# Sparse attention over latent vectors: keys and values of each head made first, scores over 64 rows, values mixed straight into a head's rows

## The chip, the core and the metric

The kernel runs on one NeuronCore of a Trainium2 chip. Its engines are TensorE (PE in the profile; its weight loads are PEld), VectorE (DVE), ScalarE (ACT), GpSimd (POOL) and SyncE (SP), whose queue issues most of the loads. Each engine works through a list of its own, in order, and waits for others by semaphores. The metric is the device time of one execution in microseconds: the median of three timed runs. One execution more is recorded with the hardware profiler, and the profile is of that one.

## The reference

The model has a first block (two layers with differential and grouped attention, feed-forward parts, and a context stream) and a second block of two layers, each with three branches side by side: a sparse attention over latent vectors, a stick-breaking attention and a matrix memory, then gates and a projection. There are 256 tokens and 1024 features, all fp32. The change is in the sparse attention alone. It has 8 heads of 64 features, of which the first 16 are rotated by position; keys and values of all heads come from one latent vector of 128 features per token. Of the keys a query may see, a separate small scoring chooses 64:

```python
def dsa_attention(q, c_kv, k_rope, iq, ik, iw, w_uk, w_uv, kv_norm_w, cos, sin):
    topk = min(INDEX_TOPK, seq // 4)                      # 64
    c_kv = rms_norm(c_kv, kv_norm_w)                      # the latent vectors, rank 128
    q_rope = partial_rope(q[..., :ROPE_DIM], cos[:, None], sin[:, None])
    q_nope = q[..., ROPE_DIM:]
    k_rope = partial_rope(k_rope, cos, sin)
    ...
    q_abs = jnp.einsum('bshn,rhn->bshr', q_nope, w_uk)
    q_cat = jnp.concatenate([q_abs, q_rope], axis=-1).astype(jnp.float32) * DSA_HEAD_DIM ** -0.5
    kv_cat = jnp.concatenate([c_kv, k_rope], axis=-1).astype(jnp.float32)

    def block(args):                                      # 128 queries
        ...
        score = jnp.einsum('bth,bths->bts', iwb, jax.nn.relu(jnp.einsum('bthd,bsd->bths', iqb, ik)))
        score = jnp.where(causal[None], score, -jnp.inf)
        _, sel = lax.top_k(score, topk)
        kv_sel = jax.vmap(lambda kv, ix: kv[ix])(kv_cat, sel)
        logits = jnp.einsum('bthf,btkf->bthk', qb, kv_sel)
        logits = jnp.where(valid[:, :, None, :], logits, -jnp.inf)
        p = jax.nn.softmax(logits, axis=-1)
        return jnp.einsum('bthk,btkr->bthr', p, kv_sel[..., :DSA_KV_RANK])

    o_lat = from_blocks(lax.map(block, ...))
    o = jnp.einsum('bshr,rhv->bshv', o_lat, w_uv)
```

## The kernel before

The second block holds features on the partitions and 256 tokens along the free axis. Every projection is made of three fp32r products per weight tile (`mm3`, L78 to L80), from a high and a low part of weight and input; `unit` makes the two parts of a weight (L60, `wh`, on ScalarE, and L61, `wl`, on VectorE) from a tile `raw` that SyncE's queue loads. `pair` makes two such units into one PSUM bank `psp`. Matmuls of the attention itself are plain fp32; in the profile each of them is two instructions of one kind, and the transposes are one each.

`hybrid(l)` is one layer. The attention's part has these steps. Narrow projections come first (`kz`, `iq`), with the rope on VectorE and GpSimd (`rope`, L439 to L442). `index_bias` makes for each half t of the queries the mask `sc` (0 for a chosen key, -1e30 elsewhere): scores `psI` (L1047), then eight rounds of MAX8 and MATCH_REPLACE8 on VectorE (L1058, L1059). Then the latent vectors `ckT` (L889 to L896, normed by `psR`) and their transpose `ckt` (`psct`, L899); the queries `dq` (two `pair`s, L902 to L907, scaled on ScalarE at L905, then the rope); and the transposed up-projections of the keys, `ukT` (`psuk`, L916).

For each cp, that is four heads, the queries are brought into the latent space: `qa` (`psqa`, L926, copied by ScalarE at L930). For each half t of the queries, with nk = 128 (t + 1) keys, the scores `psL` are a sum of two matmuls: 128 rows of `qa` against `ckT` (L940), and 64 rows of `dq` against the rotated part `kR` (L941). The index e in 0, 1 is the half of the 128 rows that a head occupies. The softmax follows: add the mask (L946), maximum (L947), exp on ScalarE (L950), reciprocal (L951), scale (L952). The probabilities are transposed (`psdt`, L958), copied by ScalarE (`dPT`, L960) and mixed with the latent vectors (`psol`, L961, 512 columns), copied by VectorE (`olat`, L963); at the end of each cp the mix goes through the up-projection of the values (`psya`, L968, two heads in two halves of the array's columns).

The order on each engine is not the order of the program: a scheduler deals the instructions out by its own costs, and fills the gaps of the attention with products of the later projections (`sbq`, `sbk`, `sbv` and others). PSUM has eight banks of 512 fp32 columns, shared out by tags in `PSUM_TAGS`: "p" two (`psp`), "s" two (`psL`, `psI`, `psol` and others), "a" one, "b" three. A new tile of a tag waits until a bank of it is read out. SBUF tiles have tags in the same way.

## Time and profile before

| | |
|---|---|
| median of three timed runs | 2602.63 us (2601.14 to 2602.85) |
| profiled execution, first to last instruction (its span) | 2598.3 us |
| TensorE busy | 2500.7 us (96%), 15175 matmuls |
| VectorE, ScalarE, GpSimd busy | 1435.2, 1038.1, 406.3 us |
| mean granted clock of TensorE | 0.984 of 2.4 GHz |
| read from HBM | 343.04 MB, 132 GB/s over the span |

The page gives no other time of the profiled execution than its span. Busy is the union of an engine's instructions; a matmul's length includes its way through the array, so successive matmuls overlap, and their cost is read from start to start. The second block begins at about 1885 us; the sparse attention of its layer 0 runs from about 1900 to 1993 us, that of layer 1 from about 2254 to 2347 us.

### The profile page before, as it was taken

The numbers are of one execution on the slowest core, as the hardware profiler recorded it, in microseconds if no ns is written. First come the engines' busy times: TensorE is split into PE (matmuls) and PEld (weight loads), VectorE is DVE, ScalarE is ACT, GpSimd is POOL, SyncE is SP. The second block draws the span as 40 slices with busy tenths as digits, with TensorE's granted clock in tenths as the row PEclk, the third lists the DMA queues.
The fourth block names the chain that finished last, engine by engine and source line by source line (L and its number), as shares of the span: only waits on it lengthen the run. The fifth ranks groups of instructions, "written<-read, shape, count | busy, mean of one in ns | idle before, by whom it ended". The sixth has DMA issues, their size and how long they took to land. (4 is left out here: it accounts for less than half of the span.)

```text
span 2598.3 us, 38082 instructions
## 1 busy us (share of the span) xinstructions
PE 2500.7 (96%) x15175; PEld 2105.4 (81%) x15175; DVE 1435.2 (55%) x2492; ACT 1038.1 (40%) x1740; POOL 406.3 (16%) x427
## 2 busy tenths in 40 slices
PE   7999999999999999999999999999989999899998
PEld 3777778666678888788888887799887999788998
DVE  4333337666565333474333477656785765676755
ACT  3222234554353222343222355644444544446443
POOL 1000016220051000150000153400330010201010
PEclk9999998999999999999999999999999999999999
DMA  8443423344432322243332243455533356433453
GB/s 282 153 154 129 147 97 99 126 148 150 149 116 86 107 97 97 98 146 114 114 101 94 98 155 125 143 182 180 161 105 113 106 158 194 140 98 114 138 187 130
DMA packets 321789, 346.56 MB, mean 133 GB/s; under 512 B 23906, under 2 KB 282568, under 8 KB 321612
## 3 DMA queue, kind: packets, MB, share of 16 engines
q1 hardware_dynamic: 320706, 343.35, 40.9%
q8 instruction: 119, 1.95, 0.3%
q10 hardware_dynamic: 906, 0.78, 0.1%
q14 instruction: 58, 0.48, 0.1%
HBM read 343.04 MB, written 1.05 MB: 132 GB/s over the span
## 5 line engine op out<-in xcount | busy, mean ns | idle before, releaser
L60 ACT CAST wh<-raw 128x1024 fp32r<-128x1024 f32 (+2 forms) x534 | 527.8, 998 | 1120.7 <-PE psg L79 554.1
L61 DVE TENSOR_TENSOR wl<-raw,wh 128x1024 fp32r<-128x1024 f32 (+2 forms) x534 | 639.4, 1203 | 549.0 <-ACT wh L60 547.0
L79 PE MATMUL psg<-xl,wh 128*128 128x512 f32 (+1 forms) x1472 | 523.6, 356 | 3.1 <-POOL xl L1295 3.0
L78 PE MATMUL psg<-xh,wh 128*128 128x512 f32 (+1 forms) x1472 | 523.3, 357 | 2.9 <-ACT xh L1322 2.3
L80 PE MATMUL psg<-xh,wl 128*128 128x512 f32 (+1 forms) x1472 | 521.4, 355 | 0.0
L78 PE MATMUL psp<-xh,wh 128*128 128x256 f32 x1248 | 357.2, 287 | 10.0 <-DVE mlu L1156 3.8
L80 PE MATMUL psp<-xh,wl 128*128 128x256 f32 x1248 | 354.5, 284 | 3.1 <-DVE wl L61 3.1
L79 PE MATMUL psp<-xl,wh 128*128 128x256 f32 x1248 | 356.7, 286 | 0.6 <-POOL xl L855 0.6
L78 PEld LDWEIGHTS psg<-xh,wh 128*128 128x128 f32 x1472 | 277.3, 189 | 59.0 <-ACT wh L60 12.6
L79 PEld LDWEIGHTS psg<-xl,wh 128*128 128x128 f32 x1472 | 278.2, 189 | 53.1 <-issue 8.1
L80 PEld LDWEIGHTS psg<-xh,wl 128*128 128x128 f32 x1472 | 278.0, 189 | 39.7 <-issue 0.8
L79 PE MATMUL psy<-gl,wh 128*128 128x512 f32 (+1 forms) x800 | 273.8, 342 | 2.6 <-DVE gl L323 2.5
L78 PE MATMUL psy<-gh,wh 128*128 128x512 f32 (+1 forms) x800 | 275.2, 344 | 0.0
L80 PE MATMUL psy<-gh,wl 128*128 128x512 f32 (+1 forms) x800 | 273.6, 342 | 0.0
L78 PEld LDWEIGHTS psp<-xh,wh 128*128 128x128 f32 x1248 | 237.3, 190 | 16.3 <-issue 5.7
L80 PEld LDWEIGHTS psp<-xh,wl 128*128 128x128 f32 x1248 | 237.6, 191 | 5.4 <-DVE wl L61 4.1
L79 PEld LDWEIGHTS psp<-xl,wh 128*128 128x128 f32 x1248 | 237.9, 191 | 4.1 <-issue 2.4
L243 POOL TENSOR_TENSOR acc<-acc,sq 128x256 f32<-128x256 f32 x70 | 56.9, 816 | 1108.2 <-ACT acc L237 1102.5
L319 DVE TENSOR_TENSOR g<-sg,psg 128x512 f32<-128x512 f32 (+1 forms) x88 | 54.5, 620 | 223.4 <-PE psg L80 223.4
L78 PEld LDWEIGHTS psy<-gh,wh 128*128 128x128 f32 x800 | 150.3, 188 | 26.4 <-ACT wh L60 5.0
L79 PEld LDWEIGHTS psy<-gl,wh 128*128 128x128 f32 x800 | 151.1, 189 | 22.7 <-DVE gl L323 3.2
L80 PEld LDWEIGHTS psy<-gh,wl 128*128 128x128 f32 x800 | 150.5, 188 | 21.6 <-issue 1.7
(473 smaller groups left out, 3651.6 us busy)
## 6 DMA issues: line engine op xcount, KB each, us to landing
raw<-in_ffn_w_in SPq DMA_DIRECT2D x88, 1024.0 KB
raw<-in_w_in SPq DMA_DIRECT2D x70, 1024.0 KB
adaw<-in_ada_w SPq DMA_DIRECT2D x240, 256.0 KB
raw<-in_ffn_w_out SPq DMA_DIRECT2D x32, 1024.0 KB
adas<-in_ada_w SPq DMA_DIRECT2D x48, 256.0 KB
raw<-in_ffn_w_out SPq DMA_DIRECT2D x16, 768.0 KB
raw<-in_da_w_in SPq DMA_DIRECT2D x12, 1024.0 KB
raw<-in_w_branch SPq DMA_DIRECT2D x24, 512.0 KB
```

The lines of the kernel that those rows point to most:

```text
L60: a = nc.scalar.copy(wh[:, 0:nk, :], r)
L61: b = nc.vector.tensor_sub(wl[:, 0:nk, :], r, wh[:, 0:nk, :].bitcast(F32))
L78: mm(ps, lhsT=wh[:, k, :], rhs=xh, start=first, stop=False)
L79: mm(ps, lhsT=wh[:, k, :], rhs=xl, start=False, stop=False)
L80: mm(ps, lhsT=wl[:, k, :], rhs=xh, start=False, stop=last)
L243: b = (eng or nc.vector).tensor_tensor(acc, acc, sq, ALU.add)
L319: nc.vector.tensor_mul(g[:, 0:width], sg[:, 0:width], pu[:, 0:width])
```

## The change

The latent vectors are no longer transposed, and queries are no longer brought into the latent space. Instead, right after `ckT` is ready, the keys of every head are made from it, `kd` (`pskd`, four matmuls of 256 columns); the weights `uk` have 16 zero columns in front of each head's 48, and VectorE adds the rotated part `kR` on its way out of PSUM, so that a head has 64 rows, two heads side by side on the 128 partitions. The values of all heads are made too, tokens on the partitions, `vd` (`psvd`, two matmuls of 512 columns, copied by ScalarE). A score `psL` is then one matmul over 64 rows. The mix goes from the transposed probabilities `PT` straight into the 64 rows of a head in `psya` (matmuls of 128 columns), for one or two blocks of keys, and one copy `ya` per cp remains. `pskd` and `psvd` take the tag "a" (one bank, with `psdt`), `psya` the tag "b". The loads of `uk` and `uv` stand before the queries' projections. The changed file also has no comments; its lines in the attention are some 7 to 14 lower.

```diff
-for _t, _n in (("p", "psp psckv"), ("s", "psL psI psR psRn psst psol"), ("a", "psrot psvec psiw psct psuk psqa psdt psya psf"),
-               ("b", "psk2 pstk psz psC psyb pscm psmS psn psyc psgt")):
+for _t, _n in (("p", "psp psckv"), ("s", "psL psI psR psRn psst psol"), ("a", "psrot psvec psiw pskd psvd psdt psf"),
+               ("b", "psk2 pstk psz psC psyb pscm psmS psn psyc psgt psya")):
...
-               ("d", "kz iq kR sc csq ck dq qa olat dPT ya"), ("e", "sbq sbk sbv sbvt yb"), ("m", "mlu mlth mlv wt hn yc"),
-               ("th", "th tho uk ukT"), ("E", "rl dE"), ("br", "bh bl"), ("mg", "mg"), ("z", "z")):
+               ("d", "kz iq kR sc csq ck dq kd vd dPT ya"), ("e", "sbq sbk sbv sbvt yb"), ("m", "mlu mlth mlv wt hn yc"),
+               ("th", "th tho uk"), ("E", "rl dE"), ("br", "bh bl"), ("mg", "mg"), ("z", "z")):
...
-        ck = self.t2("ck")
-        ckT, ckt = ck[:, 0:256], ck[:, 256:512]
+        ckT = self.t2("ck")[:, 0:256]
         nc.scalar.activation(ckT, psc[:, 0:256], AF.Identity, scale=self.col['kv_norm'][:, l:l + 1])
         nc.vector.tensor_tensor(ckT, ckT, R[:, 0:256], ALU.mult)
-        pt = self.pst("psct")
+
+        uk = self.t2("uk").rearrange("p (h n) -> p h n", n=64)
+        nc.gpsimd.memset(uk[:, :, 0:16], 0.0)
+        nc.sync.dma_start(uk[:, :, 16:64], I['w_dsa_uk_2'][l])
+        uv = self.big.tile([128, 512], F32, name="uv", tag="uv")
+        nc.sync.dma_start(uv, I['w_dsa_uv_2'][l].rearrange("r h v -> r (h v)"))
+        kd, vd = [], []
+        for cp in range(2):
+            ps = self.pst("pskd")
+            for i in range(2):
+                c = 2 * cp + i
+                nc.tensor.matmul(ps[:, i * 256:(i + 1) * 256], lhsT=uk[:, 2 * c:2 * c + 2, :].rearrange("p a b -> p (a b)"), rhs=ckT)
+            t = self.t2("kd")
+            nc.vector.tensor_tensor(v2(t), v2(ps), kR.unsqueeze(1).to_broadcast([128, 2, 256]), ALU.add)
+            kd.append(t)
         for t in range(2):
-            nc.tensor.transpose(pt[:, t * 128:(t + 1) * 128], ckT[:, t * 128:(t + 1) * 128], self.ident)
-        nc.vector.tensor_copy(ckt, pt[:, 0:256])
+            ps = self.pst("psvd")
+            nc.tensor.matmul(ps, lhsT=ckT[:, t * 128:(t + 1) * 128], rhs=uv)
+            v = self.t2("vd")
+            nc.scalar.copy(v, ps)
+            vd.append(v)
         dq = []
...
-        # up-projections of the keys, transposed, 16 zero rows in front of each head
-        uk = self.t2("uk").rearrange("p (h n) -> p h n", n=64)
-        nc.gpsimd.memset(uk[:, :, 0:16], 0.0)
-        nc.sync.dma_start(uk[:, :, 16:64], I['w_dsa_uk_2'][l])
-        uv = self.big.tile([128, 8, 64], F32, name="uv", tag="uv")
-        nc.sync.dma_start(uv, I['w_dsa_uv_2'][l])
-        pt = self.pst("psuk")
-        for c in range(4):
-            nc.tensor.transpose(pt[:, c * 128:(c + 1) * 128], uk[:, 2 * c:2 * c + 2, :].rearrange("p a b -> p (a b)"), self.ident)
-        ukT = self.t2("ukT")
-        nc.scalar.copy(ukT, pt)
         ya = []
         for cp in range(2):
-            qa = {}
-            ps = [self.pst("psqa") for e in range(2)]      # the two halves of the rows write different banks
-            for i in range(2):
-                for e in range(2):
-                    r = slice(64 * e, 64 * e + 64)
-                    nc.tensor.matmul(ps[e][:, i * 256:(i + 1) * 256], lhsT=ukT[r, (2 * cp + i) * 128:(2 * cp + i + 1) * 128],
-                                     rhs=dq[cp][r, i * 256:(i + 1) * 256])
-            for e in range(2):
-                t = self.t2("qa")
-                nc.scalar.copy(t, ps[e])
-                qa[e] = t
-            ol = [self.t2("olat") for c in range(2)]       # heads 4cp, 4cp+1 | 4cp+2, 4cp+3
+            po = self.pst("psya")
...
-                        nc.tensor.matmul(L[e][:, i, :], lhsT=qa[e][:, qs], rhs=ckT[:, 0:nk], start=True, stop=False)
-                        nc.tensor.matmul(L[e][:, i, :], lhsT=dq[cp][r, qs], rhs=kR[r, 0:nk], start=False, stop=True)
+                        nc.tensor.matmul(L[e][:, i, :], lhsT=dq[cp][r, qs], rhs=kd[cp][r, i * 256:i * 256 + nk])
...
-                po = self.pst("psol")
+                PT = []
                 for st in range(t + 1):
                     pt = self.pst("psdt")
                     for h in range(4):
                         nc.tensor.transpose(pt[:, h * 128:(h + 1) * 128], E[h % 2][:, h // 2, st * 128:(st + 1) * 128], self.ident)
-                    PT = self.t2("dPT")
-                    nc.scalar.copy(PT, pt)
-                    nc.tensor.matmul(po, lhsT=ckt[:, st * 128:(st + 1) * 128], rhs=PT, start=st == 0, stop=st == t)
-                for c in range(2):
-                    nc.vector.tensor_copy(v2(ol[c])[:, :, t * 128:(t + 1) * 128],
-                                          po[:, c * 256:(c + 1) * 256].rearrange("p (e q) -> p e q", q=128))
-            ps = self.pst("psya")
-            for cc in range(2):
-                for e in range(2):
-                    nc.tensor.matmul(ps[64 * e:64 * e + 64, cc * 256:(cc + 1) * 256], lhsT=uv[:, 4 * cp + 2 * cc + e, :],
-                                     rhs=ol[cc][:, e * 256:(e + 1) * 256])
+                    PT.append(self.t2("dPT"))
+                    nc.scalar.copy(PT[st], pt)
+                for i in range(2):
+                    for st in range(t + 1):
+                        for e in range(2):
+                            h = 2 * i + e
+                            nc.tensor.matmul(po[64 * e:64 * e + 64, i * 256 + t * 128:i * 256 + t * 128 + 128],
+                                             lhsT=vd[st][:, (4 * cp + h) * 64:(4 * cp + h + 1) * 64], rhs=PT[st][:, h * 128:(h + 1) * 128],
+                                             start=st == 0, stop=st == t)
             t = self.t2("ya")
-            nc.scalar.copy(t, ps)
+            nc.scalar.copy(t, po)
```

The scheduler deals the changed work out anew. TensorE, layer 1, from where the latent vectors are ready: before, the new queries stand between products and the scores follow them (`psct` and `psuk` are some rows ahead).

```order
L80 MATMUL psp_20820<-xh3_20137,wl_20822 128x256
L926 MATMUL psqa_20611<-dq_20526,ukT_20609 128x256 x2
L78 MATMUL psp_20820<-xh4_20138,wh_20821 128x256
L79 MATMUL psp_20820<-xl4_20146,wh_20821 128x256
L80 MATMUL psp_20820<-xh4_20138,wl_20822 128x256
L78 MATMUL psp_20820<-xh5_20139,wh_20821 128x256
L79 MATMUL psp_20820<-xl5_20147,wh_20821 128x256
L80 MATMUL psp_20820<-xh5_20139,wl_20822 128x256
L926 MATMUL psqa_20612<-dq_20526,ukT_20609 128x256 x2
L940 MATMUL psL_20623<-ck_20460,qa_20617 128x128
L941 MATMUL psL_20623<-kR_20311,dq_20526 128x128
L940 MATMUL psL_20623<-ck_20460,qa_20617 128x128
```

After the change, the keys and values stand at this place:

```order
L79 MATMUL psp_20519<-xl6_20113,wh_20524 128x256
L907 MATMUL pskd_20433<-ck_20425,uk_20428 128x256 x2
L80 MATMUL psp_20519<-xh6_20105,wl_20525 128x256
L78 MATMUL psp_20519<-xh7_20106,wh_20524 128x256
L79 MATMUL psp_20519<-xl7_20114,wh_20524 128x256
L80 MATMUL psp_20519<-xh7_20106,wl_20525 128x256
L907 MATMUL pskd_20438<-ck_20425,uk_20428 128x256 x2
L913 MATMUL psvd_20443<-uv_20431,ck_20425 128x512
L913 MATMUL psvd_20447<-uv_20431,ck_20425 128x512
L78 MATMUL psp_20750<-xh0_20099,wh_20751 128x256
L79 MATMUL psp_20750<-xl0_20107,wh_20751 128x256
```

Four products stand between the two `pskd`, none between `pskd_20438` and the two `psvd`; `psp_20750`, the next projection, begins behind them, and the scores come 22 products later.

ScalarE, layer 1, the same place: before, the queries `dq_20526` are taken out of their bank among the weights' high parts.

```order
L60 CAST wh_20821<-raw_20818 128x1024
L905 ACTIVATE dq_20526<-psp_20469 128x512
L60 CAST wh_20825<-raw_20818 128x1024
L60 CAST wh_20882<-raw_20879 128x1024
L60 CAST wh_20886<-raw_20879 128x1024
L905 ACTIVATE dq_20592<-psp_20535 128x512
L918 COPY ukT_20609<-psuk_20604 128x512
L930 COPY qa_20617<-psqa_20611 128x512
L930 COPY qa_20619<-psqa_20612 128x512
```

After the change, both copies of the values stand ahead of both queries:

```order
L60 CAST wh_20751<-raw_20748 128x1024
L60 CAST wh_20755<-raw_20748 128x1024
L60 CAST wh_20812<-raw_20809 128x1024
L60 CAST wh_20816<-raw_20809 128x1024
L915 COPY vd_20445<-psvd_20443 128x512
L915 COPY vd_20449<-psvd_20447 128x512
L921 ACTIVATE dq_20510<-psp_20453 128x512
L921 ACTIVATE dq_20576<-psp_20519 128x512
L60 CAST wh_20873<-raw_20870 128x1024
```

What moved: `dq_20510` (bank `psp_20453`) is now behind `vd_20449`, which needs the second `psvd`.

VectorE, layer 1, after `psR`: before, the rope of the first queries (L440, L442) stands among the rounds of the mask.

```order
L227 TENSOR_SCALAR dg_20457<-ident_88,rs_20451 128x128
L1058 MAX m8_20354<-sc_20324 128x8
L440 TENSOR_TENSOR trot_20528<-trot_20528,cs2_16255 128x512
L1059 MATCH_REPLACE sc_20324<-m8_20354,sc_20324 128x128
L896 TENSOR_TENSOR ck_20460<-ck_20460,psR_20453 128x256
L1058 MAX m8_20357<-sc_20324 128x8
L442 TENSOR_TENSOR dq_20526<-dq_20526,trot_20528 128x512
L1059 MATCH_REPLACE sc_20324<-m8_20357,sc_20324 128x128
L900 COPY ck_20460<-psct_20463 128x256
L1058 MAX m8_20360<-sc_20324 128x8
L61 TENSOR_TENSOR wl_20822<-raw_20818,wh_20821 128x1024
```

After the change, from the first to the second sum of the keys:

```order
L909 TENSOR_TENSOR kd_20436<-pskd_20433,kR_20276 128x512
L1049 MAX m8_20325<-sc_20289 128x8
L1167 SCALAR_TENSOR_TENSOR fg_20286<-one4_16262,ex_21799 4x256
L1050 MATCH_REPLACE sc_20289<-m8_20325,sc_20289 128x128
L61 TENSOR_TENSOR wl_20817<-raw_20809,wh_20816 128x1024
L1049 MAX m8_20328<-sc_20289 128x8
L1049 MAX m8_20352<-sc_20289 128x8
L1050 MATCH_REPLACE sc_20289<-m8_20328,sc_20289 128x128
L1050 MATCH_REPLACE sc_20289<-m8_20352,sc_20289 128x256
L1051 TENSOR_SCALAR sc_20289<-sc_20289 128x128
L1049 MAX m8_20355<-sc_20289 128x8
L909 TENSOR_TENSOR kd_20441<-pskd_20438,kR_20276 128x512
```

The second `kd` stands eleven rows behind the first, behind a weight's low part and rounds of the mask for both halves of the queries; the queries' rope has moved behind it.

## Rows read from the trace of the kernel before

**Rows 1.** The page's span and its busy times (share) and instructions by engine.
```profile
span 2598.3 us, 38082 instructions
PE 2500.7 (96%) x15175; PEld 2105.4 (81%) x15175; DVE 1435.2 (55%) x2492; ACT 1038.1 (40%) x1740; POOL 406.3 (16%) x427
```

**Rows 2.** Sums by stretch: length; busy PE, PEld, DVE, ACT, POOL; clock, DMA, GB/s.
```profile
1915.00:1946.00 31.00, 29.75 (x223) 27.16 (x221) 30.12 (x84) 16.99 (x28) 5.24 (x7) 1.00 0.45 136
1946.00:1993.00 47.00, 46.13 (x276) 34.51 (x277) 25.22 (x44) 21.19 (x47) 0.00 (x0) 1.00 0.35 105
2268.00:2300.00 32.00, 29.35 (x208) 26.91 (x206) 29.55 (x85) 13.25 (x24) 4.97 (x6) 0.95 0.40 131
```

**Rows 3.** Waits of TensorE, 1915 to 2347: waiter, releaser, us in total, times, longest.
```profile
PE psR L228 <- DVE dg L227: 3.9, 3, 1.9
PE psdt L958 <- DVE dE L952: 2.4, 2, 1.4
```

**Rows 4.** Timeline of TensorE, layer 0: start, us, line, operation, tiles, shape, count.
```profile
1909.64 0.71 PE L1047 MATMUL psI<-kz,iq 64*128 64x128 f32 x8 [1.07 <-DVE iq L442]
...
1910.74 0.28 PE L79 MATMUL psp<-xl,wh 128*128 128x256 f32 x1
1910.86 0.28 PE L80 MATMUL psp<-xh,wl 128*128 128x256 f32 x1
...
1925.13 1.13 PE L926 MATMUL psqa<-dq,ukT 64*128 64x256 f32 x4
1926.19 0.39 PE L79 MATMUL psp<-xl,wh 128*128 128x256 f32 x1
...
1928.15 0.49 PE L940 MATMUL psL<-ck,qa 128*128 128x128 f32 x2
1928.57 0.48 PE L941 MATMUL psL<-kR,dq 64*128 64x128 f32 x2
...
1948.31 1.12 PE L961 MATMUL psol<-dPT,ck 128*128 128x512 f32 x2
1949.27 0.59 PE L940 MATMUL psL<-ck,qa 128*128 128x256 f32 x2
...
1953.37 0.38 PE L79 MATMUL psp<-xl,wh 128*128 128x256 f32 x1
...
1965.37 1.08 PE L968 MATMUL psya<-olat,uv 128*64 128x256 f32 x8
...
2049.70 0.40 PE L1127 MATMUL psyb<-sbz,sbvt 128*64 128x128 f32 x4
2049.92 0.59 PE L1126 MATMUL psyb<-sbz,sbvt 128*64 128x256 f32 x2
```

**Rows 5.** Groups by line, VectorE, 1915.2 to 1946.2: busy us, mean ns, idle before.
```profile
L61 DVE TENSOR_TENSOR wl<-raw,wh 128x1024 fp32r<-128x1024 f32 x8 | 9.7, 1208 | 0.0
L1058 DVE MAX8 m<-sc 128x8 f32<-128x128 f32 (+1 forms) x16 | 5.5, 346 | 0.3 <-POOL sc L1055 0.3
L1059 DVE MATCH_REPLACE8 sc<-m,sc 128x128 f32<-128x128 f32 (+1 forms) x16 | 5.4, 336 | 0.0
L442 DVE TENSOR_TENSOR dq<-dq,trot 128x512 f32<-128x512 f32 x2 | 1.3, 672 | 0.0
```

**Rows 6.** Groups by line, ScalarE, 1915.2 to 1993.
```profile
L930 ACT COPY qa<-psqa 128x512 f32<-128x512 f32 x4 | 2.3, 586 | 4.6 <-PE psqa L926 4.6
```

**Rows 7.** Sums by 2 us around layer 1's psR.
```profile
2270.00:2272.00 2.00, 1.14 (x10) 0.93 (x8) 2.00 (x9) 0.00 (x0) 1.40 (x3) 1.00 0.55 187
2272.00:2274.00 2.00, 0.93 (x8) 0.96 (x8) 2.00 (x6) 1.05 (x1) 0.84 (x1) 1.00 0.00 1
2274.00:2276.00 2.00, 2.00 (x13) 2.00 (x12) 1.82 (x8) 0.00 (x0) 0.00 (x0) 0.60 0.00 0
2276.00:2278.00 2.00, 2.00 (x11) 2.00 (x11) 1.98 (x6) 0.00 (x0) 0.00 (x0) 0.54 0.00 0
```

**Rows 8.** Timeline of SyncE's queue, 1855 to 1935.
```profile
1885.47 0.65 SPq L911 DMA_DIRECT2D uk<-in_w_dsa_uk  x1
```

## The prediction

> **What bounds the kernel now.** I read the page first: TensorE is busy 2500.7 of 2598.3 us [rows 1]. Then the sum by stretches, for the two places where the sparse attention runs, one in each layer of the second block: in 1915 to 1946 us VectorE is busy 30.12 of 31.00 us and TensorE 29.75, in the same part of layer 1 it is 29.55 and 29.35 of 32.00; in the later part, 1946 to 1993, TensorE has 46.13 of 47.00 and VectorE only 25.22 [rows 2]. So each attention has two parts. In the first, which makes the mask of chosen keys on VectorE (MAX8 and MATCH_REPLACE8 in turn), TensorE and VectorE are both full; in the second TensorE alone is. The view of waits says that TensorE pays little for this: between 1915 and 2347 it waited 2.4 us at the transposes psdt for VectorE's dE (once in each layer, 1.4 the longest) and 3.9 at psR [rows 3]. The gaps of the attention are filled with the three products per weight (L78 to L80) of other projections, 0.12 us each from start to start [rows 4]. Hence a matmul less in the attention is time less, as long as VectorE keeps up.
>
> **What goes and comes on TensorE, per layer.** All lengths are from start to start in the timeline [rows 4]; a plain fp32 matmul shows as two instructions.
> Out: eight psqa matmuls, four pairs of 1.06 (1925.13 to 1926.19): 4.2. The scores psL for 128 keys go in steps of 0.42 per matmul (1928.15 to 1928.57), eight of them 3.3; for 256 keys from 1949.27 to 1953.37, 4.1; each twice: 14.9. Six psol of 512 columns at 0.96 (1948.31 to 1949.27): 5.8. Eight psya in two groups of 1.08: 2.2. Six transposes (psct, psuk), an estimate of 0.1 each from the 0.12 of a product: 0.6. Together 27.6 us.
> In: four pskd of 256 columns, priced like psqa (128 rows here, 64 there): two times 1.06, 2.1. Two psvd of 512 columns like psol: 1.9. Sixteen psL. The four psI matmuls for 128 keys, on alternating halves of the rows, took 0.71 (eight instructions), so the first group of 128 keys costs 0.7. In the changed order the other groups come in twos on the same half of the rows, as psqa does: 2.1 for each group of 256 keys, and by half the columns 1.1 for the second group of 128. Sum 6.0. Were all alternating, it would be 3.5; did all go like the old psL, half of its 14.9, 7.4. Twenty-four psya of 64 columns of weights and 128 moving ones: such a pair for two heads took 0.22 in psyb (2049.70 to 2049.92), twelve are 2.6, and six starts between other products at about 0.2 (what psqa and psL lose at their edges) 1.2: 3.8; with no two side by side 6.5. Together 13.9, bounds 11.4 to 17.8.
> Out less in: 13.7 us per layer, 27.4 in all (20 to 32).
> On such edges the Trainium skill has a rule that speaks against the change: "TensorEngine Tiling (Array Packing)", Key Properties, says that changing the tiling mode drains the engine. The trace agrees in kind: 0.42 per matmul where psL changes between 128 and 64 rows at every step, 0.71 for four in psI, which stay at 64 [rows 4]. By the rule alone the new psya would lose at six more edges per layer, and the old psL loses at many more of them, so the sum moves the same way.
>
> **Other engines.** Per layer VectorE loses eight copies olat and one ckt and gains two adds kd; ScalarE loses ukT and four qa copies and gains two vd copies (0.586 each [rows 6]). I cost this at nothing: ScalarE is far from full, and VectorE's olat copies stand in the second part, where it has half its time free [rows 2]. The loads of uv and uk move ahead in SyncE's queue, uk to one load behind its old place; in layer 0 uk was issued at 1885.47 [rows 8] and is wanted at about 1920, so nothing waits for it, and the raw loads behind it move by less than a microsecond.
>
> **The waits that come.** The first part was full on both engines. The changed order takes work off TensorE there and leaves VectorE's, so TensorE now waits. I follow it from psR's second matmul (time 0), with 0.12 per product.
> Layer 1. VectorE must run, before the second kd add (the order rows on VectorE), six MAX8 and five MATCH_REPLACE8 (0.35 and 0.34 each: 3.8), three wl of 1.21 (3.6), both kd adds (0.67, as the rope's add of that width, L442: 1.3) [rows 5], and ck, a scan and a threshold, by an estimate from those 1.3: 10.0 by the means, about 9 as successive ones overlap at their edges. TensorE in that time has 14 products (1.7), waits 0.5 for ck, pskd (1.1), 4 products, 0.6 for the bank, pskd (1.1): it stands at 5.5. psvd uses the one bank that pskd must leave, so TensorE waits about 3.5 us. Behind psvd in TensorE's queue is everything, the other projections' products too. Then psvd (1.0), its copy by ScalarE (0.586 and the signals) before the next psvd has the bank (0.7), psvd (1.0), and the next product needs a bank that dq0 still holds: on ScalarE dq0's evacuation stands behind both vd copies (the second one and its own, 0.6 each, with the signals 1.3). 22 products follow (2.6), and psL finds dq0's rope just done (0.3) and for 256 keys its banks just freed (0.6). Waits: 0.5+0.6+3.5+0.7+1.3+0.3+0.6 = 7.5, against the 1.0 at psdt now (2.4 less 1.4 [rows 3]): 6.5 worse. The first softmax is ready when VectorE is, and TensorE now comes to it with 70 products done instead of 146; those it runs later, in place of attention.
> Layer 0 has 11 and 10 products where layer 1 has 4 and none, so kd's add is done in time: 0.5 for ck, 0.7 between the psvd, 1.3 for dq0, 0.5 for its rope, 1.2 for banks of psL: 4.2, against 1.4 at psdt now [rows 3]: 2.8 worse.
> Second part: I added up VectorE's list there to 16 us (layer 0), against 84 products (10 us) and some 10 us of attention on TensorE; the waits are on bank copies with 6 to 8 products between them. I take no new wait, bound 0 to 4 us per layer.
> The clock. In 2270 to 2274 us TensorE was busy 1.14 and 0.93 of 2.00 us, and in 2274 to 2278 the granted clock was 0.60 and 0.54 [rows 7], that is mostly the lower of its two levels, 1.2 and 2.4 GHz. By the list above TensorE is busy 4.7 of some 11 us in layer 1's first part, so I expect the lower level there again and for longer. Another 4 to 6 us at half clock cost 2 to 3 us, less what falls into a wait anyway, and layer 0 may have some; I take 3 for both layers, bounds 0 and 8.
> Sum: 2598.3 - 27.4 + 6.5 + 2.8 + 3 = 2583.2 for the profiled span. The median of the timed runs, 2602.63, is 4.3 above the profiled span, and I carry that over: 2587.5, so 2587.
>
> **The rivals.**
> A, nothing waits anew. For it: now the same engines are full and TensorE waits 2.4 us at psdt. Against: a single bank for pskd, psvd and psdt, and ScalarE's order. 2602.6 - 27.4 = 2575.
> B, VectorE is the bound. If its first part must take the same time and its wl units come late after it, TensorE's gain turns into waits: the 9.3 above, the bound of 4 per layer in the second part (8), and products that wait for a wl of 1.2 in four places of each layer (9.6). That is 26.9 of the 27.4, 2602.6 - 0.5 = 2602. For it: 30.12 of 31.00 us. Against: the part after has VectorE half free.
> C, slower: the clock. If the waits in the first part put TensorE at 1.2 GHz for the whole way to the first softmax and through the transposes after it, about 22 us in each layer, and the work in it takes twice as long, 11 us lost each: 2587 - 3 + 22 = 2606. It ends slower from 9.3 us lost per layer on, that is some 19 us at the lower level. For it: 2.07 of 4.00 us busy went ahead of the 1.2 GHz in layer 1 [rows 7], and the new list has less. Against: the waits end after 12 us, and then products come without a gap. The Trainium skill's "TensorE: Matmul & The Clock Gate", HAM oscillation, speaks for C: an engine that waits between bursts starts every burst cold. The trace agrees for one stretch in layer 1 [rows 7] and not for 1915 to 1946, where the clock was 1.00 with 29.75 of 31.00 busy [rows 2].
> D, the halves of the rows don't run side by side, or psya's pairs don't: 17.8 instead of 13.9 per layer, 2587 + 7.8 = 2595. That the change doesn't do what it says would be this one.
>
> **How the numbers follow.** Forecast, gain less these waits: 0.60; A 0.16; D 0.09; B 0.10; C 0.05. About 0.2%, 5.2 us, is what can be told from no change. The forecast, A and D (7.6 below) end more than that below 2602.6, faster 0.85; B is the same, 0.10; C slower, 0.05. The forecast's own range is 2580 to 2594, by the bounds of the matmuls and of the second part. The whole range goes from A to half way between D and B: 2575 to 2600.
>
> **What would show it.** Right: psL's busy time in each layer near 6 us, no psol and psqa, psya near 4; waits of TensorE at psvd for VectorE's kd, longest in layer 1, then at the products behind it for ScalarE; the first psdt earlier in layer 1 than in layer 0, counted from psR; from psz on the same rows as now, 15 to 20 us earlier at the end. Wrong: psL near 8 or psya near 6.5 (D); VectorE without idle time from 1915 on for 80 us (B); two or more stretches at half clock in each attention (C); psvd without a wait (A).

## The result, and where the time went

The changed kernel takes 2581.6 us (median of four runs, 2579.63 to 2583.06), the kernel before 2601.9: a ratio of 0.9921, 95% interval 0.9907 to 0.9935. It is faster, by 20 us; 2587 was forecast and 2575 to 2600 the range. The profiled run took 2581.55 us around a span of 2579.8, 18.5 less than the span of [rows 1]. The page's span and busy times by engine, of the changed kernel:
```profile
span 2579.8 us, 37984 instructions
PE 2475.5 (96%) x15131; PEld 2091.2 (81%) x15131; DVE 1429.9 (55%) x2478; ACT 1036.1 (40%) x1734; POOL 406.6 (16%) x427
```
TensorE is busy 25.2 us less. The 12,744 products of the weights (L78 to L80) run in the same order in both kernels, so the start of the same product in two traces tells where time was gained, provided that both kernels have run the same other matmuls up to it. For each layer I take the product in front of psI and the one 373 products later, behind the first sixteen instructions of psz. In layer 1, first the kernel before, then the changed one:
```profile
2260.86 0.28 PE L78 MATMUL psp<-xh,wh 128*128 128x256 f32 x1
...
2350.82 0.28 PE L79 MATMUL psp<-xl,wh 128*128 128x256 f32 x1
```
```profile
2252.23 0.28 PE L78 MATMUL psp<-xh,wh 128*128 128x256 f32 x1
...
2334.59 0.28 PE L79 MATMUL psp<-xl,wh 128*128 128x256 f32 x1
```
The first starts 8.6 us earlier than before, the second 16.2: 7.6 gained in that attention. In layer 0 the same two products go from 1.15 us later to 9.17 earlier: 10.3 gained. So 17.9 us come from the two attentions; all the rest of the program, where nothing was changed, is 0.6 shorter.

The stretches that answer to the first and the third of [rows 2] (columns as there):
```profile
1916.00:1947.00 31.00, 26.26 (x188) 22.96 (x187) 30.23 (x85) 14.29 (x23) 5.31 (x7) 1.00 0.47 129
2259.00:2291.00 32.00, 25.09 (x145) 19.83 (x144) 29.41 (x85) 10.63 (x17) 4.29 (x7) 0.84 0.32 99
```
VectorE is as full as before, TensorE no longer is: 26.26 and 25.09 us where it had 29.75 and 29.35, and in layer 1 the granted clock is down to 0.84. The first part of an attention is now VectorE's. The waits of TensorE between 1916 and 2330 (columns as in [rows 3]):
```profile
PE psvd L913 <- DVE kd L909: 3.3, 1, 3.3
PE psR L228 <- DVE dg L227: 2.9, 3, 1.4
...
PE psp L78 <- ACT dq L921: 2.3, 2, 1.2
PE psL L934 <- DVE dE L939: 2.1, 3, 1.1
...
PE psvd L913 <- ACT vd L915: 1.4, 2, 0.7
...
PE psL L934 <- DVE dq L442: 0.9, 1, 0.9
...
PE pskd L907 <- DVE kd L909: 0.6, 1, 0.6
```
The transposes psdt, which waited 2.4 us for dE, are gone from the list; psvd stands at its head. The place is in layer 1, on TensorE's timeline (start, us, line, operation, tiles, shape, count, and in brackets the idle time before it with what ended it):
```profile
2268.37 1.13 PE L907 MATMUL pskd<-ck,uk 128*128 128x256 f32 x4 [0.56 <-DVE kd L909]
2272.76 2.08 PE L913 MATMUL psvd<-uv,ck 128*128 128x512 f32 x2 [3.26 <-DVE kd L909]
2275.52 2.07 PE L913 MATMUL psvd<-uv,ck 128*128 128x512 f32 x2 [0.68 <-ACT vd L915]
2278.76 0.58 PE L78 MATMUL psp<-xh,wh 128*128 128x256 f32 x1 [1.17 <-ACT dq L921]
```
From 2266 to 2279 one single bank is handed on: pskd, pskd, psvd, psvd, each after the one before it has been read out. VectorE, which has to empty it, is not idle meanwhile; between the two kd adds it runs a weight's low part and rounds of the mask:
```profile
2267.64 0.68 DVE L909 TENSOR_TENSOR kd<-pskd,kR 128x512 f32<-128x512 f32 x1
...
2269.27 1.20 DVE L61 TENSOR_TENSOR wl<-raw,wh 128x1024 fp32r<-128x1024 f32 x1
2270.41 0.60 DVE L1049 MAX8 m<-sc 128x8 f32<-128x128 f32 x2
...
2272.05 0.66 DVE L909 TENSOR_TENSOR kd<-pskd,kR 128x512 f32<-128x512 f32 x1
```
Behind the wait TensorE is slow. Sums by 2 us of the same place (length; PE, PEld, DVE, ACT, POOL; clock, DMA, GB/s), as in [rows 7]:
```profile
2268.00:2270.00 2.00, 1.13 (x4) 0.68 (x4) 2.00 (x6) 0.78 (x1) 0.00 (x0) 1.00 1.04 365
2270.00:2272.00 2.00, 0.00 (x0) 0.00 (x0) 2.00 (x9) 0.00 (x0) 0.14 (x1) 1.00 0.26 25
2272.00:2274.00 2.00, 1.24 (x2) 0.50 (x2) 2.00 (x7) 0.00 (x0) 0.15 (x1) 0.57 0.99 335
...
2280.00:2282.00 2.00, 2.00 (x11) 2.00 (x11) 2.00 (x4) 0.00 (x0) 0.91 (x1) 0.50 0.00 0
2282.00:2284.00 2.00, 2.00 (x18) 1.74 (x18) 2.00 (x7) 0.00 (x0) 0.48 (x1) 0.87 0.00 0
```
No matmul runs from 2270 to 2272; from 2272 the granted clock is 0.50 (1.2 GHz) until 2282, about 10 us; before it was some 3.5 us there [rows 7]. A psvd of 512 columns takes 2.08 us, where psol, of the same shape, took 1.12 [rows 4].

The busy time of psL and then of psya, each in layer 0 (1916 to 1990) and layer 1 (2259 to 2340; PE, PEld and the engines that read it):
```profile
1916.00:1990.00 74.00, 6.51 (x32) 4.15 (x32) 4.27 (x8) 0.00 (x0) 1.00 0.47 132
2259.00:2340.00 81.00, 5.94 (x32) 3.86 (x32) 4.27 (x8) 0.00 (x0) 0.94 0.38 118
...
1916.00:1990.00 74.00, 3.95 (x48) 2.50 (x48) 0.00 (x0) 1.18 (x2) 1.00 0.47 132
2259.00:2340.00 81.00, 3.95 (x48) 2.50 (x48) 0.00 (x0) 1.18 (x2) 0.94 0.38 118
```
"psL near 6, psya near 4" was the mark of the forecast; 8 and 6.5 would have been rival D.

### The profile page after: what moved, and what is told of

Its sections match the earlier page's. It is cut to its first block, busy times and chain, and to the rows that moved or that the text cites. A ratio compares the mean times of both kernels' runs of the same rounds, so it can differ in the third digit from the quotient of the medians.

```text
span 2579.8 us, 37984 instructions
## 1 busy us (share of the span) xinstructions
PE 2475.5 (96%) x15131; PEld 2091.2 (81%) x15131; DVE 1429.9 (55%) x2478; ACT 1036.1 (40%) x1734; POOL 406.6 (16%) x427
## 5 line engine op out<-in xcount | busy, mean ns | idle before, releaser
L78 PE MATMUL psg<-xh,wh 128*128 128x512 f32 (+1 forms) x1472 | 523.0, 357 | 2.9 <-ACT xh L1313 2.3
L80 PE MATMUL psg<-xh,wl 128*128 128x512 f32 (+1 forms) x1472 | 521.4, 355 | 0.0
L78 PE MATMUL psp<-xh,wh 128*128 128x256 f32 x1248 | 356.6, 286 | 11.9 <-DVE mlu L1147 3.8
L80 PE MATMUL psp<-xh,wl 128*128 128x256 f32 x1248 | 353.9, 284 | 3.2 <-DVE wl L61 3.2
L78 PEld LDWEIGHTS psg<-xh,wh 128*128 128x128 f32 x1472 | 277.3, 189 | 59.0 <-ACT wh L60 12.6
L80 PEld LDWEIGHTS psg<-xh,wl 128*128 128x128 f32 x1472 | 278.2, 189 | 39.7 <-issue 0.8
L78 PE MATMUL psy<-gh,wh 128*128 128x512 f32 (+1 forms) x800 | 275.3, 344 | 0.0
L80 PE MATMUL psy<-gh,wl 128*128 128x512 f32 (+1 forms) x800 | 273.8, 342 | 0.0
L78 PEld LDWEIGHTS psp<-xh,wh 128*128 128x128 f32 x1248 | 236.8, 190 | 20.7 <-issue 5.5
L80 PEld LDWEIGHTS psp<-xh,wl 128*128 128x128 f32 x1248 | 236.9, 190 | 5.0 <-DVE wl L61 4.0
L78 PEld LDWEIGHTS psy<-gh,wh 128*128 128x128 f32 x800 | 150.4, 188 | 26.3 <-ACT wh L60 5.0
L80 PEld LDWEIGHTS psy<-gh,wl 128*128 128x128 f32 x800 | 150.5, 188 | 21.7 <-issue 1.7
```

Source lines behind the costliest of these rows:

```text
L78: mm(ps, lhsT=wh[:, k, :], rhs=xh, start=first, stop=False)
L80: mm(ps, lhsT=wl[:, k, :], rhs=xh, start=False, stop=last)
```

## The experiments

My theory after the result: the matmuls saved are as counted, and what is lost is lost in the first part of each attention, to the single bank of pskd and psvd (with the clock behind it) and to ScalarE's order. Its rival: VectorE sets when the first softmax is there, so a wait taken away only comes back elsewhere. Twelve runs were made, each with the kernel before beside it on its chip (medians 2599.27, 2598.18, 2599.76; 2598.97 for the last). The table gives the ratio to before with its interval, and from each profile the difference in us to the kernel before: in the two attentions, by the starts of the same products (minus is a gain), and in the rest of the program.

| kernel | ratio (95%) | layer 0 | layer 1 | rest |
|---|---|---|---|---|
| changed | 0.9921 (0.9907-0.9935) | -10.3 | -7.6 | -0.6 |
| changed, again | 0.9936 (0.9924-0.9949) | -10.3 | -7.7 | +2.9 |
| e1 banks | 0.9896 (0.9881-0.9911) | -11.8 | -14.2 | -1.6 |
| e2 vd late | 0.9913 (0.9896-0.9931) | -12.7 | -10.9 | +1.4 |
| e3 psL alternating | 0.9941 (0.9924-0.9959) | -10.4 | -8.1 | +3.2 |
| e4 scores alone | 0.9940 (0.9923-0.9958) | -6.6 | -8.2 | -2.6 |
| e5 banks, vd late | 0.9897 (0.9882-0.9912) | -12.8 | -15.8 | -2.1 |
| e11 the same again | 0.9891 (0.9878-0.9905) | -12.6 | -15.8 | -0.5 |
| e6 with psL's banks | 0.9907 (0.9890-0.9923) | -13.0 | -16.1 | +3.6 |
| e7 values alone | 1.0032 (1.0007-1.0056) | +9.3 | +8.6 | -3.4 |
| e12 values alone, one run | - | +0.1 | +8.6 | +0.5 |
| e8 psya's halves | 0.9945 (0.9930-0.9960) | -10.0 | -7.6 | +0.4 |
| e9 kd off VectorE | 0.9918 (0.9904-0.9931) | -11.0 | -12.9 | +4.8 |

The attention's gain of one and the same kernel repeats within 0.2 us (changed, e5), as long as the granted clock does the same in it (e7 and e12 are the exception); the rest moves by several us from run to run. It goes with the clock too: outside the two attentions TensorE had 1.2 GHz for 69 us in e7's profile, 80 in that of the kernel before, 95 in e9's. So the columns by layer tell more than the ratio of one kernel, and I read them first.

**e1, the banks.** 

> One edit on the changed kernel: pskd and psvd take the three banks of tag b instead of the single bank of tag a. Theory (a bank that waits for VectorE): in layer 1 TensorE's waits at psvd for VectorE's kd (3.3 us), at the second pskd (0.6) and at the second psvd in both layers (1.4 together) go, 5.3 us, and with them most of the half-clock stretch behind them (2273 to 2282), another 2 to 3; part of it comes back at psL, which waits for VectorE's dE. 2581.6 less 5 to 8: 2574 to 2577. Rival (VectorE sets when the first softmax is there, so what TensorE gains it waits for at psL and psdt): 2581 to 2582.


```
-               ("a", "psrot psvec psiw pskd psvd psdt psf"),
-               ("b", "... psgt psya"):
+               ("a", "psrot psvec psiw psdt psf"),
+               ("b", "... psgt psya pskd psvd"):
```
Measured 2572.48 us, ratio 0.9896, and in layer 1 6.6 us more gain than the changed kernel, in layer 0 1.5. Waits of TensorE in e1's attentions and the middle of the program (1914 to 2325), and its sums by 2 us at the place of the old wait:
```profile
PE psL L934 <- DVE dE L939: 4.6, 4, 1.8
...
PE psL L934 <- DVE dq L442: 1.0, 1, 1.0
...
PE psp L78 <- ACT dq L921: 0.7, 1, 0.7
```
```profile
2266.00:2268.00 2.00, 1.29 (x7) 0.74 (x6) 2.00 (x10) 1.73 (x4) 0.00 (x0) 1.00 0.32 106
...
2270.00:2272.00 2.00, 0.99 (x9) 0.78 (x7) 2.00 (x5) 1.04 (x1) 0.50 (x1) 1.00 0.00 0
...
2274.00:2276.00 2.00, 1.43 (x13) 1.23 (x11) 2.00 (x5) 0.00 (x0) 0.40 (x1) 1.00 0.00 0
2276.00:2278.00 2.00, 1.34 (x7) 1.23 (x8) 2.00 (x7) 0.00 (x0) 0.00 (x0) 1.00 0.00 0
```
The waits for kd and vd are gone, and so is the stretch at 1.2 GHz: the granted clock stays 1.00 although TensorE is busy only 1.0 to 1.4 of 2.0 us in several of these. The rival is right in part: psL's waits for dE grow from 2.1 to 4.6. In layer 0 of the same run the clock fell where the changed kernel kept it, for some 3.4 us, behind psL's waits for dE (3.0 us in that layer). The 1.5 us of gain are what is left with that loss:
```profile
1944.00:1946.00 2.00, 0.96 (x6) 0.84 (x7) 1.77 (x5) 1.61 (x4) 0.00 (x0) 0.91 0.00 0
1946.00:1948.00 2.00, 2.00 (x10) 1.78 (x8) 1.63 (x4) 1.17 (x4) 0.00 (x0) 0.50 0.01 4
```
The bank is shown as the cause of the long wait in layer 1, and the low clock there as its consequence: all four profiles with the single bank and psvd ahead of dq (changed, e3, e8, e10) have the 3.3 us wait and 10.2 us at 1.2 GHz behind it, the three that move pskd and psvd to tag "b" and leave psL and kd's sum as they were (e1, e5, e11) have neither. (e6 and e9, on tag "b" too, have no such wait, and 3.4 us at 1.2 GHz some us later.)

**e2, vd behind dq.** 

> One edit on the changed kernel: psvd and its copies vd stand behind the two projections dq in the program, so that ScalarE takes dq0 out of its bank before the copies vd. Theory (ScalarE's order): the two waits of products for dq's evacuation, 2.3 us together, and layer 0's wait of 0.9 for dq's rope go, and the wait at psvd for kd in layer 1 (3.3) stays or shrinks, as products now stand ahead of psvd: 2576 to 2579. Rival (the waits only move, since psvd still needs the one bank): 2581 to 2582.


```
-        for t in range(2):          # psvd and its copy vd, ahead of dq
-            ps = self.pst("psvd")
-            ...
         dq = []
         for j in range(2):
             ...
+        for t in range(2):
+            ps = self.pst("psvd")
+            ...
```
Ratio 0.9913, by itself not apart from 0.9921; by layer 2.4 and 3.3 us more gain. No product waits for dq's evacuation any more; the psvd wait stays (1916 to 2325):
```profile
PE psvd L920 <- DVE kd L909: 2.9, 1, 2.9
```
So ScalarE's order was a cause of its own, in both layers, and the wait for kd another. (In layer 1 part of the gain is the clock: 6.8 us at 1.2 GHz instead of 10.2.)

**e3, psL held to alternate.** 

> One edit on the changed kernel: the four psL matmuls of a group are held in the program's order, so that successive ones use different halves of the rows; in the changed kernel the groups for 256 keys come in twos on the same half. Theory (halves run side by side only when they alternate): psL's time per layer from start to start falls from 5.8 towards 3.5, 4.6 us for both layers, 2577; where a group's second bank comes late, products fill in as before. Rival (the halves do not overlap, or the order makes psL wait for both banks): 2582 to 2585.


```
-   nc.tensor.matmul(L[e][:, i, :], lhsT=dq[cp][r, qs], ...)
+   was, mm = mm, nc.tensor.matmul(L[e][:, i, :], lhsT=dq[cp][r, qs], ...)
+   if was:
+       self.behind(mm, was)
```
As the rival said, next to no gain: 0.1 and 0.5 us by layer, and the ratio 0.9941 does not differ beyond its interval. The starts of psL's matmuls in layer 0 say why; first e3, then the changed kernel:
```profile
1937.09 0.70 PE L935 MATMUL psL<-kd,dq 64*128 64x256 f32 x2 [1.12 <-DVE dE L942]
1938.26 1.13 PE L935 MATMUL psL<-kd,dq 64*128 64x256 f32 x6
```
```profile
1938.15 1.85 PE L934 MATMUL psL<-kd,dq 64*128 64x256 f32 x8 [1.12 <-DVE dE L939]
```
Three alternating matmuls take 1.13 us where four in twos took 1.85, so the halves do run side by side. But the order makes the group wait for the second bank after its first matmul: three products run in between, and a group cut in two pays its edge twice. In layer 0 psL's own time falls from 6.0 to 5.2 us, and the products take 0.5 more.

**e4, the scores part alone.** 

> The scores part of the change alone: kd and the single 64-row psL, but the mix by way of the latent vector as before (psct, psol, olat, psya of 256 columns); no psvd, no vd. Theory (the gain lies in the scores): against the kernel before, psqa 4.2, psuk 0.4 and 9 us of psL go and pskd 1.6 comes, 12 us per layer, less waits for VectorE's kd of 0.6 to 2 per layer: 2579 to 2582, the same as the whole change. Rival (the values part carries its share, a quarter of the gain or more): 2586 or more.


```
-            ps = self.pst("psvd") ...              # no vd
+        pt = self.pst("psct") ...                  # ckt, psol, olat and
+            po = self.pst("psol") ...              # 256-column psya as before
```
Measured 2583.43 us, ratio 0.9940: by the ratio that is the rival's mark (2586 of 2601.9), with the theory's 2582 at the edge of the interval. By the traces 14.8 of the changed kernel's 17.9 us in the attentions come with the scores alone. Layer 1 is even 0.6 ahead of the whole change: without psvd TensorE waited 1.3 us for kd in the two layers, with it 3.9. Layer 0 is 3.7 behind; in e4 it has 3.4 us at 1.2 GHz (from 1934), up to 1.7 us, which the changed kernel does not have. So the share of the values is small by the attentions, 3 us of 18; the ratio alone can't tell it from a quarter.

**e7 and e12, the values part alone.** 

> The values part of the change alone: psvd, the copies vd and the 24 psya of 128 columns; the scores as before (psuk, psqa, psL in two parts). Theory (the gain lies in the scores): psol 5.2, psya 2.0 and psct go, psvd 1.9 and psya 3.5 come, and psdt, now among psya, loses 0.7: 1.2 us per layer, less waits at psvd's single bank; 2600 to 2603 of 2602, ratio 0.999 to 1.000. Rival (the parts share the gain): below 0.997.

 

> The values part alone, profiled once more, since its ten runs lay in two groups (2596 to 2602 and 2609 to 2622 us). Theory (the groups differ by the stretches at 1.2 GHz in the attentions): if this run is of the lower group, the granted clock is 1.00 or nearly so from 1925 to 1950 and from 2290 to 2316, and the attentions are 1 to 3 us shorter than before; if it is of the upper group, both stretches are at 0.50 again, 20 us each. Rival (the groups differ elsewhere): low clock in the attentions of a run of the lower group too.


```
-            ps = self.pst("pskd") ...              # no kd
+        pt = self.pst("psuk") ...                  # ukT, psqa, qa, and
+   nc.tensor.matmul(L[e][:, i, :], lhsT=qa[e][:, qs], ..., stop=False)
+   nc.tensor.matmul(L[e][:, i, :], lhsT=dq[cp][r, qs], ..., start=False)
```
Slower: 1.0032 (1.0007 to 1.0056), outside what both sides expected. The ten runs lie in two groups, five from 2595.9 to 2601.6 and five from 2608.7 to 2622.1. The profiled one (2614.5) is of the second, and the run profiled later (2609.26) too. Sums by 4 us of layer 0 and one of its psL matmuls, in the first profile and then in the second:
```profile
1924.00:1928.00 4.00, 2.91 (x19) 2.21 (x17) 3.07 (x12) 1.42 (x3) 1.38 (x2) 1.00 0.21 69
1928.00:1932.00 4.00, 4.00 (x11) 2.49 (x11) 3.33 (x8) 0.59 (x1) 1.27 (x1) 0.51 0.00 0
...
1944.00:1948.00 4.00, 4.00 (x16) 3.35 (x16) 0.96 (x1) 1.04 (x1) 0.00 (x0) 0.50 0.00 0
...
1940.53 1.22 PE L942 MATMUL psL<-ck,qa 128*128 128x256 f32 x2
```
```profile
1928.00:1932.00 4.00, 2.90 (x18) 2.20 (x17) 3.06 (x14) 1.29 (x3) 1.26 (x2) 1.00 0.19 65
1932.00:1936.00 4.00, 4.00 (x20) 2.77 (x19) 3.88 (x8) 0.58 (x1) 1.26 (x1) 1.00 0.00 0
...
1938.91 0.70 PE L942 MATMUL psL<-ck,qa 128*128 128x256 f32 x2
```
The same instructions behind the same wait of 1.1 us: once the clock falls and stays at 1.2 GHz for 20 us, in which TensorE is never idle and does psqa and psL with two products among them and sixteen behind, once it stays at 2.4. The first costs 9.3 us against before, the second 0.1; layer 1 fell to 0.50 in both profiles (+8.6 each). The ten runs' mean granted clocks fit: 0.984 to 0.986 in the lower group, 0.976 to 0.980 in the upper. From the difference of the groups' means, 0.007, I estimate 35 us more at 1.2 GHz, which cost 18 us, and the groups' medians, 2596.8 and 2614.9, are 18 us apart. So the two groups differ by the clock; that it is the clock in the attentions is shown for two profiles of the upper group, and a run of the lower one was not profiled. This is rival C's mechanism and price (11 us a layer) in another kernel. Without the low clock the values part gains nothing in layer 0.

**e5 and e6, the two edits together, and psL's banks.** 

> Both edits that gained: pskd and psvd on the three banks of tag b, and psvd with its copies behind the projections dq in the program. With the banks alone 0.7 us of waits for dq's evacuation and 1.0 for dq's rope were left, and 4.6 at psL for VectorE's dE. Theory (the two causes are separate): 1 to 2 us below the kernel with the banks alone (ratio 0.9896 to before), 0.989. Rival (VectorE sets the first softmax; the waits for dE grow by what the others lose): 0.9896 again.

 

> The two edits together, and psL's groups for 256 keys on tag b, so that they do not wait until VectorE's dE has emptied the two banks of the groups for 128 keys. Theory (4.6 us at psL for dE are a matter of banks): ratio to before 0.988 or 0.9875. Rival (VectorE is full there until the first softmax; the wait moves from psL to the transposes psdt): as with the two edits alone, 0.989.

 e6 adds:
```
-  L = [self.pst("psL")[:, 0:2 * nk] ...
+  L = [self.pst(("psL", "psM")[t])[:, 0:2 * nk] ...   # psM on tag "b"
```
e5: 0.9897, 0.9 and 1.6 us by layer beyond e1; the interval alone couldn't tell. In layer 1 that is what was expected of separate causes: the waits for dq's evacuation and rope, 1.7 in e1, are 0.2. In layer 0 e1 had no such wait, and the 0.9 goes with the low clock, which e1 has there and e5 does not. Of the waits in the attention psL for dE is left at 5.0 us in all. e6: another 0.3 in each layer, no more: psL's waits for dE shrink to 3.1 us and 2.3 come at psdt, as the rival said; and layer 1 has some 3.4 us at 1.2 GHz again (from 2279), up to 1.7 us, where e5 had none. But a group of psM goes through in one piece and alternating, eight instructions in 1.07 us (to the next product at 1951.66) instead of 1.78 in the changed kernel (1938.15 to 1939.93):
```profile
1950.59 1.13 PE L934 MATMUL psM<-kd,dq 64*128 64x256 f32 x8
1951.66 0.39 PE L78 MATMUL psp<-xh,wh 128*128 128x256 f32 x1
```

**e8, psya's pairs.** 

> One edit on the changed kernel: psya's order for the second tile of queries, both key tiles of one head before those of the other, so that two successive matmuls write the same half of the rows in 16 of the 24 per layer. Theory (the two halves of psya's rows run side by side, as 0.146 us per pair says): up to 2.3 us per layer more, 4 us in all, ratio 0.993 to 0.994 instead of 0.992. Rival (they do not, and the price is set by the length of one): no change.


```
-   for st in range(t + 1):
-       for e in range(2):
+   for e in range(2):
+       for st in range(t + 1):
```
psya's 48 instructions take 4.37 us busy per layer instead of 3.95, and the attentions lose 0.3 and 0.0, a small part of what the theory allowed. But the edit did less than its text says: where the first head's second matmul meets the second head's first, the two are on different halves again, and 20 of the 24 matmuls per layer still start together with another, within 0.02 us. Four run alone. One of these, to the next product, and then two heads' matmuls in the changed kernel:
```profile
1955.45 0.43 PE L958 MATMUL psya<-dPT,vd 128*64 128x128 f32 x2
1955.82 0.39 PE L80 MATMUL psp<-xh,wl 128*128 128x256 f32 x1
```
```profile
1956.76 0.44 PE L958 MATMUL psya<-dPT,vd 128*64 128x128 f32 x4
1957.12 0.39 PE L80 MATMUL psp<-xh,wl 128*128 128x256 f32 x1
```
One matmul takes 0.37 us, two take 0.36: the halves do run side by side. Four single ones cost the 0.42, so by this all 24 would cost some 2.5 (an estimate), and D's price for them, 6.5 less 3.8, stands. The ratio, 0.9945, isn't told apart from the changed kernel's.

**e9, kd taken off VectorE.** 

> The kernel with both edits (banks, vd late), and kd's sum taken off VectorE: ScalarE copies pskd out of its bank (0.586 us each) and GpSimd adds kR. Theory (VectorE is full from psR to the first softmax and sets when psL gets its banks back): VectorE loses two adds of 0.67 per layer, the waits of psL for dE (5.0 us in all) shrink by 1.3 per layer or a little less: 2 us, ratio to before 0.989. Rival (VectorE is not the limit; ScalarE's two copies now stand ahead of dq0's evacuation and GpSimd's add is slower): no change, 0.9897, or up to 2 us slower, 0.9905.


```
-  nc.vector.tensor_tensor(v2(t), v2(ps), kR..., ALU.add)
+  nc.scalar.copy(t, ps)
+  nc.gpsimd.tensor_tensor(v2(t), v2(t), kR..., ALU.add)
```
Worse than e5 in both layers (by 1.7 and 3.0): the wait for dE shrinks to 2.2 us, and a longer one for the queries' rope takes its place (1916 to 2325):
```profile
PE psL L935 <- DVE dq L442: 4.8, 2, 3.3
...
PE psL L935 <- DVE dE L940: 2.2, 2, 1.8
```
In layer 1 ScalarE empties dq0 at 2270.84, behind both copies kd, and VectorE takes up its rope at 2275.03, with other work between. Two things more are in the loss: both attentions have some 3.4 us at 1.2 GHz (from 1940.6 and 2278.5), up to 1.7 us each, where e5 has none; and VectorE did not gain the time of the two adds, for while GpSimd adds (2270.22 to 2272.92) its L1169 and L1170 take 1.24 and 1.50 us; the same two took 0.40 and 0.66 in the changed kernel. So this run doesn't test the theory: how much time VectorE lacks by itself stays open.

**e10 and e11, both again on one chip.** 

> The changed kernel itself again, beside the two versions that came out ahead, on their chip: ratio to before 0.992 as before (0.9907 to 0.9935).

 

> The kernel with both edits (banks, vd late) again in five rounds, beside the changed kernel on one chip: 5 to 7 us below the changed kernel, ratio to before 0.9895 to 0.99. If the gain over the changed kernel were the chance of one chip, 0.9915 or more.

 The changed kernel 2582.35 us, e11 2571.04: the version with both edits beats both kernels, by 11 us (5 to 7 were expected) and by 29 us. Of the 11, 10.5 are in the two attentions.

## Why the prediction was right

The measured 2581.6 us lies in the range, near the lower edge of the forecast's own 2580 to 2594. In its terms, per layer in us (start to start in the timeline, between the two products of the section on the result):

| step | predicted | layer 0 | layer 1 |
|---|---|---|---|
| the attention's own matmuls | -13.7 | -13.5 | -12.7 |
| products and other matmuls beside them | 0 | -0.1 | -0.6 |
| new waits, less those that went | +2.8, +6.5 | +3.2 | +3.7 |
| the clock | +3 in both together | 0 | +2.0 |
| sum | -15.1 in both together | -10.3 | -7.6 |

**Own matmuls: right.** psL takes 6.0 and 5.5 us (6.0 predicted), psya 3.5 (3.8), psvd and pskd 3.7, and 4.1 in layer 1 without the clock (4.0), by the prices of psqa, psI, psol and psyb. What went was a little less than summed: psol took 5.4 and 4.8, not 5.8. Not in the sum was psdt, which now alternates with psya: 24 instructions take 2.6 us instead of 2.3 and 1.9.

**Waits: the mechanism right, the size in layer 1 too large.** In layer 1 psvd waits 3.3 for the second kd add (3.5 predicted), psvd behind psvd 0.7 (0.7), the product behind dq0's copies 1.2 (1.3), the second pskd for the bank 0.6 (0.6): each is there, the longest in layer 1, as in the list. The waits for ck (0.5) and the rope (0.3) didn't come, psL's was 0.3 (0.6). That makes 4.9 where 6.5 stood. The table has 3.7, because psR in front of the attention waits 0.9 where it waited 1.9, and psqa's 0.2 went with it; the sum had neither. In layer 0 the rope and psL came longer than predicted, 0.9 and 1.8 (0.5 and 1.2). Layer 1's waits are 2.8 of the 3.4 us by which the span is shorter than 2583.2, and the clock 1.0; the other terms nearly cancel. The mark "first psdt earlier in layer 1" held: 26.1 us behind psR there, 29.1 in layer 0.

**The clock: right in place, 2.0 instead of 3.** psvd loses 1.9 us and the products behind it 1.75, less the 1.7 that the kernel before lost there.

**The 4.3 us around the span: wrong.** Around every later profiled run it is 1.7 to 2.0. I had subtracted the span of one run from the median of others, so the term held the difference of two runs; 2.5 us of the 5.4 by which the forecast is high.

**The rivals.** A fell: 10.5 us of new waits came, where 2.4 went. D fell by psL's and psya's times; its bound of 17.8 adds up to 18.0 from its terms, and e8 leaves its price as it was. B is half true: VectorE was full and decided where TensorE waited, but the gain did not vanish, since the products left over run in the second part. C didn't happen in this kernel, and happened in full in e7; 0.05 was too little for a mechanism that another order brings about, in one run and not in the next. That layer 0 kept its clock here was luck, as far as these runs show: e1, e4 and e9 have some 3.4 us at 1.2 GHz there. The Trainium skill's "TensorE: Matmul & The Clock Gate", Part 1, says that the clock follows how busy the engine has lately been; e1 and the changed kernel agree for layer 1 (without matmuls from 2270 to 2272, then 0.50; none such in e1, and 1.00), e7 does not by the profile's busy time: 4.00 of 4.00 us at 0.50.

## What to carry to other kernels

Where matmuls are taken out of a stretch that two engines fill, list in the new order what the other engine must finish first; here the time came back as a wait at the first tile that shares a single bank, and in layer 1 another bank cured it (e1). Look at the bank of every new tile and at what the evacuating engine has in front of it before counting a saving. And compare two traces of a planned program by the starts of the same products, at places up to which both have done the same other work, and look at the granted clock in each stretch before giving a difference to an edit: that told 0.3 us apart where whole runs differ by several.

## What the chip showed that I had not expected

- The clock of TensorE can stay at 1.2 GHz for 20 us while the engine is busy all the time (e7: 4.00 of 4.00 us, granted 0.50; psqa, psL and two products, then products alone), and the same instructions can run at 2.4 GHz in another run (e12, layer 0): 9.1 us between them.
- It can also stay at 2.4 GHz with TensorE busy 0.99 to 1.97 of each 2.00 us for 8 us on end (e1, layer 1), and fall in the same run after 1.25 and 0.96 of 2.00 us (layer 0, 1942 to 1946). These busy times don't tell which of the two comes.
- Eight 64-row instructions of 256 columns take 1.07 us if the halves of the rows alternate and 1.78 if they come in twos. Two psya matmuls on different halves of the columns take as long as one (0.36 and 0.37 us).
- VectorE's instructions can take more than twice their time while GpSimd adds (e9: 1.24 and 1.50 us for 0.40 and 0.66).
